# Convolution sums of VectorE in PSUM, and three tiles convolved on TensorE with streamed tap matrices of two token phases

## The chip, the cores and the metric

The kernel runs on one core of one Trainium2 chip. The metric is the device time of one execution in microseconds; less is better.

## What is computed

Two transformer blocks over 512 tokens of 1024 channels, in float32. The change lies in the second layer of the first block, a conformer convolution:

```python
def conformer_conv(h, w_pw1, b_pw1, w_dw, b_dw, ln_g, ln_b, w_pw2, b_pw2):
    u = h @ w_pw1 + b_pw1
    a, g = jnp.split(u, 2, axis=-1)
    u = a * jax.nn.sigmoid(g)
    u = depthwise_conv(u, w_dw) + b_dw
    u = jax.nn.silu(layer_norm(u, ln_g, ln_b))
    return u @ w_pw2 + b_pw2
```

The depthwise convolution has 31 taps along the tokens and its own weights for each channel. Before it stand an attention mixer and a squared-relu MLP, behind it another MLP and the second block with its gated MLP; they are the same in both kernels.

## The kernel before

Channels stand on the 128 partitions and the 512 tokens on the columns, so a tensor of 1024 channels is eight tiles. Each float32 operand of a product is split into a 12 bit head and the exact rest; a product of 128 input and 128 output channels is three TensorE instructions (`mm3`, L336 to L338): head by head, head by rest, rest by head.

Weights come from memory in the order of a plan (`make_plan`), packed into blocks of 512 columns; a load on SP's queue (L251) brings two blocks, 512 KB. ScalarE writes the head of each block (L264), VectorE the rest (L265), four blocks ahead of the one in use. Three buffers hold raw loads and nine hold split blocks. A raw buffer is free again when VectorE has split both its blocks.

The conformer's first product, `pw1`, gives two tiles of sums for each channel tile c, the value and the gate (24 instructions of 512 columns each); those of tiles 0 and 1 are computed in the part before. `glu` (L1131) evacuates them: two VectorE multiplications by the norm (L1136, L1137, one input in PSUM), a sigmoid on ScalarE, and one VectorE instruction that adds a bias and multiplies (L1139). Its result, with 15 zeros at each end, is convolved in one of four ways, by the letter in `CONV`:

- V (tiles 0, 2, 3): 31 VectorE instructions (L1087, then L1091), each of which multiplies the shifted input by a weight per partition and adds it to the sum. Input and sum are in SBUF.
- P (tiles 1, 4): for each tap ScalarE multiplies (L1102) and GpSimd adds (L1103), both in SBUF.
- M (tile 5): 10 taps as P and 21 as V into another buffer, and a VectorE addition of the two (L1171) at the end.
- E (tiles 6, 7): on TensorE. A tap is a diagonal matrix of 128 by 128, in head and rest, and 31 taps of three instructions of 512 columns add up in one bank of PSUM (`conv_pe` L1107 makes the head and rest of the input, L1109 and L1110, and `run_pe` L1114 issues the products). GpSimd writes the diagonals of tile 6 during the MLP before (L1056), ScalarE those of tile 7 as they are used (L1060).

V and P taps are background work: lists of closures of which a fixed number is issued at certain places of the program, from at most two tiles of a list in turn (`tick`, L318). `TICK = (5, 4)` is issued after each `pw1` product from tile 2's gate on (11 times): 5 taps of VectorE, 4 of ScalarE and GpSimd. `TICK2` is issued after every eight taps in `run_pe`. What is left comes after it (`drain`). Each engine works its instructions off in the order in which they were placed, so a split of weights stands behind the taps that were issued before it. PSUM has eight banks of 512 columns; all sums take theirs from these.

Behind the convolution comes the layer norm in halves of the tokens: TensorE sums all eight tiles over the partitions (`means`, L1179, in the order of `LN_ORDER`), ScalarE evacuates, VectorE subtracts, ScalarE squares, TensorE sums the squares (L1195).

Of the kernel before, what the change touches and what calls it, by code (L numbers as in the profile page):

```python
# [21 lines left out]
T = 512  # L22
# [10 lines left out]
CONV = "VPVVPMEE"  # L33
MIX = 10
TICK2 = (9, 5)
# [28 lines left out]
# ---------------------------------------------------------------- host layout  # L64


def vec_layout():
    cols, n = {}, 0
    for name, width in (("g", 64), ("sc", 12), ("qn", 3), ("kvn", 2), ("bp1", 16), ("dw", 248),
                        ("bdw", 8), ("lng", 8), ("lnb", 8), ("bp2", 8), ("n1", 8), ("n2", 8),  # L70
                        ("qn2", 1), ("kn2", 1), ("ps", 4), ("ifr", 1), ("sgn", 1)):
# [85 lines left out]
def pack(plan):  # L157
    """Cuts the plan into blocks of up to 512 columns, and those into loads of two blocks, but for the first two."""
# [7 lines left out]
    return [blocks[:1], blocks[1:2]] + [blocks[i:i + 2] for i in range(2, len(blocks), 2)]  # L166


def host_arrays(a):
# [7 lines left out]
    flat = lambda m: m.reshape(m.shape[0], -1)  # L177
    m = {
        "a": np.concatenate([win[:, 1536:2176], kr, kr, kr, krs], 1),
# [33 lines left out]
    ], 1)  # L213
# [10 lines left out]
# ---------------------------------------------------------------- chip  # L224


class Weights:
    """Streams the weight blocks in and splits each into a 12 bit head and the exact rest."""
# [40 lines left out]
    def more(self, limit):  # L269
        """Splits one block beyond what is due, up to a number of blocks ahead."""  # L270
# [12 lines left out]
class Program:  # L283
# [10 lines left out]
    # -- storage  # L294
# [23 lines left out]
    def tick(self, n, n2):  # L318
        """Background work: n and n2 operations of the two lists of queues, from a list's first two in turn."""
# [13 lines left out]
    # -- arithmetic  # L333
# [6 lines left out]
    def units(self, name, t, xs, ks=None):  # L340
        """One closure (ps, columns) per product of a weight piece."""
# [13 lines left out]
    def kouter(self, names, h, ps=None, cols=slice(0, T), hooks=None, extra=None, ks=None):  # L355
        """Several output tiles at once, an input tile after the other."""
# [13 lines left out]
    def split(self, p, src, scale=None, cols=T, rows=slice(0, 128)):  # L370
        """p = (head, rest) of src [* scale per partition]."""
# [12 lines left out]
    def rsqrts(self, jobs):  # L384
        """out = (s / n + eps) ** -0.5, with one Newton step, for each (s, n, out)."""
# [23 lines left out]
    # -- tables of the scalar engine  # L409
# [4 lines left out]
    def tables(self, name):  # L414
        """Has the scalar engine load a set of tables, behind the functions that need the one before."""
# [10 lines left out]
    def fn(self, name, **args):  # L426
        """An activation whose function needs a set of tables."""
# [6 lines left out]
    def colsum(self, acc, cols=T):  # L434
        """Sums of acc over the partitions, on every partition."""
# [19 lines left out]
    # -- constants  # L455
# [13 lines left out]
    def late_consts(self):  # L469
# [14 lines left out]
        # a query on the partitions, a key on the columns: later keys are out  # L484
# [4 lines left out]
        # a key on the partitions, a query on the columns: 32 queries before the first 96 keys,  # L489
        # which stand above the 32 keys before them  # L490
# [6 lines left out]
        # a key of the last 32 on the first partitions, a query on the columns  # L497
# [4 lines left out]
        # adds the second 32 partitions to the first  # L502
# [11 lines left out]
    def angles(self):  # L514
        """cos and sin of the rope angles, row p for frequency p % 16."""
# [23 lines left out]
    # -- attention parts that both blocks use  # L539
# [7 lines left out]
    def v_tile(self, ps, rows, scales=None):  # L547
        """Values of four (block, head) groups as [v | ones | v | ones ...], head and rest."""
# [19 lines left out]
    def max_rows(self, mx, q, rows):  # L568
        """Puts the negative of the row maxima (mx[:, 4 * head + block]) into a row of each q."""
# [61 lines left out]
    def normalise(self, e, o):  # L631
        """Values of a pair of heads over their sums: the even head is on top of its sums, the odd below."""
# [5 lines left out]
        # the negative of 1 / s, with one Newton step  # L638
# [8 lines left out]
    def head_ops(self, job, ys, nslots):  # L647
        """Closures for the scores and for the values of the slots of all heads; job(n) gives head n."""
# [20 lines left out]
    def parts(self, name, t, xs, done, ks=None, step=2):  # L669
        """A product in closures of a few input tiles each; done(sums) runs after the last."""  # L670
# [15 lines left out]
    # -- block 1, layer 0, mixer  # L686
    def mla(self, first):
# [10 lines left out]
        # products of constants until the first data is there: they raise the array's clock  # L698
# [68 lines left out]
        # shared key rope on partitions 64..95  # L767
# [6 lines left out]
        # query rope, (head, frequency) on the partitions  # L774
# [15 lines left out]
        # rows of a head: (64 | rope 32 | -max or 1 | zeros) or (-max or 1 | zeros | rope 32 | 64)  # L790
# [203 lines left out]
    # -- squared relu mlp  # L994
# [45 lines left out]
    # -- conformer convolution  # L1040
    def diagonals(self, c, early):
        """The taps of a channel tile as diagonal matrices, head and rest: at once, or eight as they are used."""
        nc = self.nc
        w = self.vec[:, self.V["dw"] + 31 * c:self.V["dw"] + 31 * c + 31]
        wh = self.cpool.tile([128, 32], F32R, name=f"wh{c}")
        wl = self.cpool.tile([128, 32], F32, name=f"wl{c}")
        nc.vector.tensor_copy(out=wh[:, :31], in_=w)
        nc.vector.tensor_sub(out=wl[:, :31], in0=w, in1=wh[:, :31].bitcast(F32))

        def eight(t0):  # L1050
            n = min(8, 31 - t0)
            pl = []
            for ww in (wh.bitcast(F32), wl):
                p = self.wide(F32R).rearrange("p (t c) -> p t c", c=128)
                if early:
                    nc.gpsimd.tensor_mul(out=p[:, :n], in0=self.ident[:, None, :].to_broadcast([128, n, 128]),  # L1056
                                         in1=ww[:, t0:t0 + n][:, :, None].to_broadcast([128, n, 128]))
                else:
# [17 lines left out]
    def conformer(self, x, h, ps4, rs, first):  # L1076
# [37 lines left out]
        def run_pe():  # L1114
            groups = [(i, t0) for i in range(len(late)) for t0 in range(0, 31, 8)]
            d, sums = {}, {}
            for n, (i, t0) in enumerate(groups):
# [4 lines left out]
                if t0 == 0:  # L1122
                    sums[i] = self.PS()
# [619 lines left out]
```

## Time and profile before

| | before |
|---|---|
| median of 3 timed runs | 1869.91 us (1869.52 to 1872.47) |
| span of the profiled execution | 1867.9 us |
| mean granted TensorE clock | 0.973 |
| TensorE busy | 1773.1 us, 95% |
| VectorE busy | 1176.0 us, 63% |
| ScalarE busy | 828.6 us, 44% |
| GpSimd busy | 330.1 us, 18% |

The profiled execution has its span as its time; it lies 2.0 us below the median of the timed runs. In the profile PE is TensorE's products and PEld its weight loads, DVE is VectorE, ACT ScalarE, POOL GpSimd and SP the engine whose queue issues the loads. A row of the timeline has the start and the duration in us, the engine, the line, the operation, the output and input tiles and how many instructions it merges; one of the lines by shape has the count, then busy us and mean ns of one, then the idle time before. [...]

### The profile page before, as it was taken

The page shows a single profiled execution, that of the slowest core. Times are in us where ns is not written, and L with a number is a line of the kernel's source. Part 1 is how long each engine was busy: PE and PEld are TensorE (multiplying, and loading weights), DVE is VectorE, ACT ScalarE, POOL GpSimd, SP SyncE. Part 2 cuts the span into 40 slices and gives each one's busy share as a digit, 9 for nine tenths or more (in the row PEclk, how much of TensorE's full clock was granted, in tenths as well). Part 3 has the DMA queues.
Part 4 walks back from the last instruction along what each step waited for, and adds up shares of the span by engine and source line. Part 5 has one row for each costly group of instructions (what it writes and reads, how often), then busy time and mean ns, then how long its engine had stood idle before and what let it go on. Part 6 is the DMA issues. An engine that isn't in the chain of part 4 may idle for free.

```text
span 1867.9 us, 22812 instructions
## 1 busy us (share of the span) xinstructions
PE 1773.1 (95%) x8630; PEld 1459.5 (78%) x8630; DVE 1176.0 (63%) x1786; ACT 828.6 (44%) x1531; POOL 330.1 (18%) x353
## 2 busy tenths in 40 slices
PE   9999979999999986839999999999999999999999
PEld 7778877888888865729888888887777888888887
DVE  7978695344444899985934443458988654344442
ACT  6546645333333544817644242436666433232231
POOL 3413270000000357820300000015122200000000
PEclk9999999999999998969999999999999999999999
DMA  5231313322222211002232232223221332332231
GB/s 200 70 96 50 102 46 113 99 93 90 101 92 79 86 39 55 14 22 69 91 100 94 90 102 90 93 87 104 59 81 53 117 102 90 94 98 91 93 99 57
DMA packets 47581, 158.83 MB, mean 85 GB/s; under 512 B 6592, under 2 KB 7040, under 8 KB 47472
## 3 DMA queue, kind: packets, MB, share of 16 engines
q1 hardware_dynamic: 45472, 152.31, 24.9%
q0 software_dynamic: 1936, 5.07, 0.9%
q8 instruction: 67, 1.10, 0.2%
q14 instruction: 42, 0.34, 0.1%
q10 hardware_dynamic: 64, 0.02, 0.0%
HBM read 149.86 MB, written 4.19 MB: 82 GB/s over the span
## 4 chain that ended last, share of the span: by engine, by line
PE 72%; DVE 20%; issue 3%; ACT 2%; POOL 1%; DMA 1%; SPq 0%; POOLq 0%; DVEq 0%; ACTq 0%
PE ps L337 23%; PE ps L336 23%; PE ps L338 23%; DVE P L1091 5%; DVE W L265 2%; DVE P L947 1%; DVE P L380 1%; DVE S L1091 1%; PE ps L602 1%; POOL P L950 1%; DVE S L1479 1%; ACT S L429 1%; DVE P L377 1%; DVE S L403 1%; PE ps L1195 1%
## 5 line engine op out<-in xcount | busy, mean ns | idle before, releaser
L338 PE MATMUL ps<-P,W 128*128 128x512 f32 (+1 forms) x2413 | 900.0, 373 | 16.6 <-DVE W L265 16.6
L337 PE MATMUL ps<-P,W 128*128 128x512 f32 (+1 forms) x2413 | 900.6, 373 | 8.5 <-DVE P L380 8.5
L336 PE MATMUL ps<-P,W 128*128 128x512 f32 (+1 forms) x2413 | 904.7, 375 | 2.2 <-ACT P L379 1.0
L265 DVE TENSOR_TENSOR W<-raw,W 128x512 fp32r<-128x512 f32 x546 | 399.0, 739 | 396.1 <-ACT W L264 391.9
L264 ACT ACTIVATE W<-raw 128x512 fp32r<-128x512 f32 x546 | 338.6, 629 | 681.0 <-PE ps L338 583.8
L338 PEld LDWEIGHTS ps<-P,W 128*128 128x128 f32 x2413 | 458.2, 190 | 105.4 <-DVE W L265 19.4
L337 PEld LDWEIGHTS ps<-P,W 128*128 128x128 f32 x2413 | 458.7, 190 | 95.1 <-DVE P L380 10.0
L336 PEld LDWEIGHTS ps<-P,W 128*128 128x128 f32 x2413 | 458.6, 190 | 90.2 <-ACT P L379 1.6
L950 POOL TENSOR_TENSOR P<-P 128x256 f32<-128x256 f32 x48 | 46.6, 979 | 798.7 <-DVE P L947 797.6
L377 DVE TENSOR_TENSOR P<-S,P 128x512 fp32r<-128x512 f32 (+1 forms) x130 | 91.0, 706 | 50.1 <-ACT P L376 49.3
L1103 POOL TENSOR_TENSOR P<-P,S 128x512 f32<-128x512 f32 x69 | 113.8, 1670 | 49.0 <-ACT S L1102 47.6
L1091 DVE SCALAR_TENSOR_TENSOR P<-P,vec 128x512 f32<-128x512 f32 x90 | 112.3, 1288 | 0.0
L376 ACT ACTIVATE P<-S 128x512 fp32r<-128x512 f32 (+1 forms) x130 | 78.9, 613 | 70.2 <-DVE S L1666 25.8
L1008 DVE SCALAR_TENSOR_TENSOR S<-ps,S 128x512 f32<-128x512 f32 x64 | 43.7, 690 | 37.3 <-PE ps L338 37.1
L379 ACT ACTIVATE P<-P,vec 128x256 fp32r<-128x256 f32 (+1 forms) x80 | 43.7, 550 | 50.3 <-POOL P L950 30.4
L449 POOL TENSOR_TENSOR S<-S 128x256 f32<-128x256 f32 (+1 forms) x45 | 48.1, 1070 | 76.3 <-ACT S L448 73.9
L380 DVE SCALAR_TENSOR_TENSOR P<-P,vec 128x256 fp32r<-128x256 f32 (+1 forms) x80 | 55.9, 712 | 8.3 <-ACT P L379 8.2
L336 PE MATMUL ps<-P 128*128 128x512 f32 (+4 forms) x134 | 53.0, 395 | 7.3 <-ACT P L1060 3.3
L337 PE MATMUL ps<-P 128*128 128x512 f32 (+4 forms) x134 | 53.3, 398 | 4.2 <-DVE P L1110 3.8
L338 PE MATMUL ps<-P 128*128 128x512 f32 (+4 forms) x134 | 52.9, 395 | 1.6 <-ACT P L1060 1.6
L615 POOL TENSOR_TENSOR P<-S,P 128x512 fp32r<-128x512 f32 (+1 forms) x24 | 34.3, 1428 | 112.5 <-DVE P L614 95.6
L448 ACT ACTIVATE S<-P 128x256 f32<-128x256 f32 (+1 forms) x105 | 46.4, 472 | 17.4 <-DVE P L1035 11.4
(270 smaller groups left out, 1464.2 us busy)
## 6 DMA issues: line engine op xcount, KB each, us to landing
raw<-in_w SPq DMA_DIRECT2D x270, 512.0 KB
P<-in_xT SPq DMA_DIRECT2D x8, 256.0 KB
P<-in_xT POOLq DMA_DIRECT2D x8, 256.0 KB, 5.7
keep<-P SPq DMA_DIRECT2D x8, 256.0 KB
P<-P SPq DMA_DIRECT2D x16, 128.0 KB
P<-keep POOLq DMA_DIRECT2D x8, 256.0 KB, 4.9
out<-P SPq DMA_DIRECT2D x7, 256.0 KB
raw<-in_w SPq DMA_DIRECT2D x2, 256.0 KB
```

The lines of the kernel that those rows point to most:

```text
L264: nc.scalar.activation(out=w[:, 0, :cols], in_=r, func=AF.Copy)
L265: nc.vector.tensor_sub(out=w[:, 1, :cols], in0=r, in1=w[:, 0, :cols].bitcast(F32))
L336: mm(ps, w[0], x[0], start=first, stop=False)
L337: mm(ps, w[0], x[1], start=False, stop=False)
L338: mm(ps, w[1], x[0], start=False, stop=last)
L376: nc.scalar.activation(out=hi, in_=src, func=AF.Copy)
L377: nc.vector.tensor_sub(out=lo, in0=src, in1=hi.bitcast(F32))
L380: nc.vector.scalar_tensor_tensor(out=lo, in0=src, scalar=scale, in1=hi.bitcast(F32), op0=OP.mult, op1=OP.subtract)
L449: (eng or nc.vector).tensor_add(out=acc, in0=acc, in1=t)
L950: ins = eng.tensor_add(out=x[k][:, cols], in0=x[k][:, cols], in1=m[k][:, cols]).ins
L1091: V.scalar_tensor_tensor(out=dst, in0=u, scalar=w, in1=dst, op0=OP.mult, op1=OP.add)
L1103: G.tensor_add(out=dst, in0=dst, in1=p)
```

## The change

- VectorE's sums (tiles V) are kept in a bank of PSUM; the last tap writes the result to SBUF.
- Tile 5 goes from M to E, so TensorE convolves three tiles, VectorE three, and GpSimd with ScalarE two.
- The E tiles use other matrices. The 128 partitions hold 64 channels at odd and at even tokens (two phases), and a matrix carries, for each pair of an input and an output phase, the tap that leads from the one to the other. 16 matrices, each on 256 columns, do the 31 taps of 64 channels. They are made on the host and come through the stream of weights between `pw1` and `pw2` (96 pieces of 128 columns). The diagonals, made on GpSimd and ScalarE, are gone.
- For that, the last step of `glu` of an E tile is four VectorE instructions of 64 partitions and 256 columns that read every second token, and its evacuation is four ScalarE instructions.
- `TICK2` goes from (9, 5) to (4, 2), issued after each of 12 groups of eight steps in place of eight groups of up to eight taps.

```diff
-CONV = "VPVVPMEE"
+CONV = "VPVVPEEE"
-TICK2 = (9, 5)
+TICK2 = (4, 2)
+EVEN_ODD = [c for c in range(8) if CONV[c] == "E"]
...
+    for i in range(2 * len(EVEN_ODD)):
+        kin("taps", i, range(16))
     kouter([("pw2", t) for t in range(4)])
...
+def tap_matrices(w):
+    m = np.zeros((16, 2, 64, 2, 64), np.float32)
+    ch = np.arange(64)
+    for s in range(16):
+        for a in range(2):
+            for b in range(2):
+                if 0 <= 2 * s + a - b < 31:
+                    m[s, a, ch, b, ch] = w[2 * s + a - b]
+    return m.reshape(16 * 128, 128)
...
         def conv_dve(c, up, dst, taps, bias):
...
                 if t == taps[0]:
+                    acc = box["acc"] = self.PS()
                     if bias:
-                        V.tensor_scalar(out=dst, in0=u, scalar1=w, scalar2=self.v("bdw", c), op0=OP.mult, op1=OP.add)
+                        V.tensor_scalar(out=acc, in0=u, scalar1=w, scalar2=self.v("bdw", c), op0=OP.mult, op1=OP.add)
...
-                    V.scalar_tensor_tensor(out=dst, in0=u, scalar=w, in1=dst, op0=OP.mult, op1=OP.add)
+                    acc = box["acc"]
+                    V.scalar_tensor_tensor(out=dst if dst is not None and t == taps[-1] else acc, in0=u, scalar=w,
+                                           in1=acc, op0=OP.mult, op1=OP.add)
...
-        def conv_pe(c, up):
-            uh, ul = self.wide(F32R)[:, :542], self.wide(F32R)[:, :542]
-            A.activation(out=uh, in_=up[:, :542], func=AF.Copy)
-            V.tensor_sub(out=ul, in0=up[:, :542], in1=uh.bitcast(F32))
+        def conv_pe(c, a, g):
+            up = self.wide(F32)[:, :544].rearrange("p (h t) -> p h t", h=2)
+            uh, ul = (self.wide(F32R)[:, :544].rearrange("p (h t) -> p h t", h=2) for _ in range(2))
+            G.memset(up[:, :, 0:8], 0.0)
+            G.memset(up[:, :, 263:272], 0.0)
+            a, g = (x.rearrange("p (t f) -> p f t", f=2) for x in (a, g))
+            for i in range(2):
+                r = slice(64 * i, 64 * i + 64)
+                for o, f, t in ((slice(0, 64), 1, 8), (slice(64, 128), 0, 7)):
+                    V.scalar_tensor_tensor(out=up[o, i, t:t + 256], in0=a[r, f], scalar=self.v("bp1", c)[r],
+                                           in1=g[r, f], op0=OP.add, op1=OP.mult)
+            A.activation(out=uh, in_=up, func=AF.Copy)
+            V.tensor_sub(out=ul, in0=up, in1=uh.bitcast(F32))
             late.append((c, uh, ul))
 
         def run_pe():
...
+            for i, (c, uh, ul) in enumerate(late):
+                sums = self.PS().rearrange("p (h t) -> p h t", h=2)
+                for g in range(2):
+                    for s in range(16):
+                        self.mm3(sums[:, g], W("taps", s, 2 * i + g), (uh[:, g, s:s + 256], ul[:, g, s:s + 256]),
+                                 s == 0, s == 15)
+                        if s % 8 == 7:
+                            self.tick(*TICK2)
+                out = vv[c].rearrange("p (t f) -> p f t", f=2)
+                for g in range(2):
+                    for b in range(2):
+                        r = slice(64 * b, 64 * b + 64)
+                        A.activation(out=out[64 * g:64 * g + 64, b], in_=sums[r, g], func=AF.Identity,
+                                     bias=self.v("bd2", 2 * i + g)[r])
...
-        with self.tc.issue_after(self.last_update):
-            self.conv_weights()
```

## Rows read from the trace of the kernel before

**Rows 1.** The page, part 4: the chain that ended last, by line.

```profile
PE ps L337 23%; PE ps L336 23%; PE ps L338 23%; DVE P L1091 5%; DVE W L265 2%; DVE P L947 1%; DVE P L380 1%; DVE S L1091 1%; PE ps L602 1%; POOL P L950 1%; DVE S L1479 1%; ACT S L429 1%; DVE P L377 1%; DVE S L403 1%; PE ps L1195 1%
```

**Rows 2.** Stretches: length, busy PE, PEld, DVE, ACT, POOL, PE clock, DMA share, GB/s.

```profile
660.00:670.00 10.00, 10.00 (x45) 8.10 (x44) 10.00 (x9) 7.23 (x12) 8.23 (x10) 1.00 0.00 0
690.00:700.00 10.00, 8.26 (x35) 6.42 (x35) 10.00 (x12) 4.25 (x7) 4.50 (x6) 1.00 0.17 52
810.00:820.00 10.00, 0.00 (x0) 0.00 (x0) 10.00 (x17) 0.00 (x0) 0.00 (x0) 0.50 0.00 0
860.00:870.00 10.00, 10.00 (x78) 9.64 (x77) 5.63 (x10) 8.89 (x17) 0.00 (x0) 1.00 0.59 177
```

**Rows 3.** Lines by shape, 640 to 830 us: count, busy us, mean ns, idle before.

```profile
L1103 POOL TENSOR_TENSOR P<-P,S 128x512 f32<-128x512 f32 x69 | 113.8, 1670 | 49.0 <-ACT S L1102 47.6
L1091 DVE SCALAR_TENSOR_TENSOR P<-P,vec 128x512 f32<-128x512 f32 x90 | 112.3, 1288 | 0.0
L265 DVE TENSOR_TENSOR W<-raw,W 128x512 fp32r<-128x512 f32 x30 | 27.7, 950 | 0.1
L1136 DVE TENSOR_TENSOR S<-ps,S 128x512 f32<-128x512 f32 x8 | 5.4, 678 | 0.0
L1060 ACT ACTIVATE P<-ident,wh 128x128 fp32r<-128x128 f32 x31 | 9.5, 387 | 0.0
```

**Rows 4.** Timeline of VectorE: start us, us, line, operation.

```profile
661.49 1.80 DVE L1091 SCALAR_TENSOR_TENSOR P<-P,vec 128x512 f32<-128x512 f32 x1
...
804.95 1.75 DVE L1091 SCALAR_TENSOR_TENSOR S<-P,vec,S 128x512 f32<-128x512 f32 x1
806.62 0.74 DVE L1091 SCALAR_TENSOR_TENSOR P<-P,vec 128x512 f32<-128x512 f32 x1
807.28 0.74 DVE L1091 SCALAR_TENSOR_TENSOR S<-P,vec,S 128x512 f32<-128x512 f32 x1
...
827.15 0.68 DVE L1171 TENSOR_TENSOR P<-P,S 128x512 f32<-128x512 f32 x1
```

**Rows 5.** Timeline of VectorE and GpSimd, 742 to 753 us.

```profile
742.87 3.44 DVE L265 TENSOR_TENSOR W<-raw,W 128x512 fp32r<-128x512 f32 x2
...
749.95 3.05 POOL L1103 TENSOR_TENSOR P<-P,S 128x512 f32<-128x512 f32 x1 [2.51 <-ACT S L1102]
...
750.57 1.28 DVE L265 TENSOR_TENSOR W<-raw,W 128x512 fp32r<-128x512 f32 x2
...
751.77 0.67 DVE L1136 TENSOR_TENSOR S<-ps,S 128x512 f32<-128x512 f32 x1
...
752.38 0.67 DVE L1137 TENSOR_TENSOR S<-ps,S 128x512 f32<-128x512 f32 x1
```

**Rows 6.** Timeline of TensorE, products of 256 columns and a weight load.

```profile
644.05 0.28 PE L336 MATMUL ps<-P,W 128*128 128x256 f32 x1
...
644.17 0.28 PE L337 MATMUL ps<-P,W 128*128 128x256 f32 x1
644.17 0.19 PEld L338 LDWEIGHTS ps<-P,W 128*128 128x128 f32 x1
```

**Rows 7.** Timeline and chain, 827 to 852 us: means (L1179) and squares (L1195).

```profile
827.28 2.07 PE L1179 MATMUL ps<-P,onesf 128*128 128x256 f32 x4 [19.86 <-DVE P L1091]
...
830.86 6.64 PE L1195 MATMUL ps<-S,onesf 128*128 128x256 f32 x16 [1.50 <-ACT S L1194]
...
848.65 3.50 PE ps L1195 x16
```

**Rows 8.** VectorE's lines by shape: forms near the new ones.

```profile
L380 DVE SCALAR_TENSOR_TENSOR P<-ps,vec,P 128x512 fp32r<-128x512 f32 x4 | 2.8, 747 | 0.0
...
L947 DVE SCALAR_TENSOR_TENSOR P<-P,vec,S 128x256 f32<-128x256 f32 x1 | 0.5, 472 | 0.0
```

**Rows 9.** Waits from 650 to 832 us (total, times, longest), and GpSimd's timeline.

```profile
POOL P L1103 <- ACT S L1102: 47.6, 11, 19.1
...
262.21 2.08 POOL L1056 TENSOR_TENSOR P<-ident,wh 128x1024 fp32r<-128x1024 f32 x1
```

More of the change, by code (lines that the diff above doesn't have):

```diff
@@ L177, in host_arrays @@
     flat = lambda m: m.reshape(m.shape[0], -1)
+    dw, bdw = f("odd_w_dw")[0], f("odd_b_dw")[0]
+    halves = [slice(128 * c + 64 * g, 128 * c + 64 * g + 64) for c in EVEN_ODD for g in range(2)]
     m = {
+        "taps": np.concatenate([tap_matrices(dw[:, r]) for r in halves], 1),
         "a": np.concatenate([win[:, 1536:2176], kr, kr, kr, krs], 1),
@@ L212, in host_arrays @@
         np.tile(np.repeat(np.array([-1.0, 1.0], np.float32), 16), 4)[:, None],
-    ], 1)
+    ] + [np.tile(bdw[r], 2)[:, None] for r in halves], 1)
     return {
@@ L1038, in mlp @@
         return self.boundary(x, m, macc, last, gi, nxt, first, extra)
[L1041 to L1058, printed above, removed]
-                    for i in range(n):
-                        nc.scalar.activation(out=p[:, i], in_=self.ident, func=AF.Copy,
-                                             scale=ww[:, t0 + i:t0 + i + 1])
-                pl.append(p)
-            return [(pl[0][:, i], pl[1][:, i]) for i in range(n)]
-        if early:
-            d = sum([eight(t) for t in range(0, 31, 8)], [])
-            self.diag[c] = lambda t0: d[t0:t0 + 8]
-        else:
-            self.diag[c] = eight
-    def conv_weights(self):
-        self.diag = {}
-        for n, c in enumerate(c for c in range(8) if CONV[c] == "E"):
-            self.diagonals(c, n == 0)
     def conformer(self, x, h, ps4, rs, first):
         nc = self.nc
-        V, A, G, mm = nc.vector, nc.scalar, nc.gpsimd, nc.tensor.matmul
+        V, A, G, mm, W = nc.vector, nc.scalar, nc.gpsimd, nc.tensor.matmul, self.W
         vv = self.pairs()
@@ L1082, in conv_dve @@
         def conv_dve(c, up, dst, taps, bias):
+            box = {}
             def tap(t):
@@ L1112, in conv_pe @@
             late.append((c, uh, ul))
         def run_pe():
-            groups = [(i, t0) for i in range(len(late)) for t0 in range(0, 31, 8)]
-            d, sums = {}, {}
-            for n, (i, t0) in enumerate(groups):
-                for g in groups[:n + 3]:
-                    if g not in d:
-                        d[g] = self.diag[late[g[0]][0]](g[1])
-                c, uh, ul = late[i]
-                if t0 == 0:
-                    sums[i] = self.PS()
-                for j, dd in enumerate(d[i, t0]):
-                    t = t0 + j
-                    self.mm3(sums[i], dd, (uh[:, t:t + T], ul[:, t:t + T]), t == 0, t == 30)
-                self.tick(*TICK2)
-                if t0 == 24:
-                    A.activation(out=vv[c], in_=sums[i], func=AF.Identity, bias=self.v("bdw", c))
+            for i, (c, uh, ul) in enumerate(late):
[12 more added lines that the diff above has]
+                                     bias=self.v("bd2", 2 * i + g)[r])
@@ L1138, in glu @@
             self.fn(SIGMOID, out=g, in_=g, func=AF.Sigmoid, bias=self.v("bp1", 8 + c))
+            if CONV[c] == "E":
+                return conv_pe(c, a, g)
+            up = self.wide(F32)
+            G.memset(up[:, 0:15], 0.0)
+            G.memset(up[:, 527:542], 0.0)
             V.scalar_tensor_tensor(out=up[:, 15:527], in0=a, scalar=self.v("bp1", c), in1=g,
@@ L1143, in glu @@
             elif CONV[c] == "V":
-                self.bg.append(conv_dve(c, up, vv[c], range(31), True))
-            elif CONV[c] == "M":
-                part = self.S()[:, :T]
+                self.bg.append(conv_dve(c, up, vv[c], range(31), True)[0])
+            else:
                 self.bg2.append(conv_pool(c, up, vv[c], range(MIX)))
-                self.bg.append(conv_dve(c, up, part, range(MIX, 31), False))
+                taps, part = conv_dve(c, up, None, range(MIX, 31), False)
+                self.bg.append(taps)
                 mixed.append((c, part))
-            else:
-                conv_pe(c, up)
         za = self.PS()
@@ L1170, in conformer @@
         for c, part in mixed:
-            V.tensor_add(out=vv[c], in0=vv[c], in1=part)
+            V.tensor_add(out=vv[c], in0=part["acc"], in1=vv[c])
         self.tables(RSQRT)
```

9 lines of the change are left out of this document (3 added, 6 removed).

## The prediction

> **What bounds the kernel now.** I read the page's chain by line first: TensorE's three product lines carry 23% each, and the largest VectorE line is the tap of the convolution, L1091, with 5% and 1% [rows 1]. Then the stretches around those taps: from 661 to 827 us VectorE is busy in every microsecond, while TensorE falls to 8.26 of 10 us at 690 and to nothing at 810 [rows 2]. So this stage is VectorE's, and what the change is worth is read there; elsewhere TensorE bounds and nothing is touched.
>
> Why VectorE is so long there is in the lines by shape and the timeline. A tap has a mean of 1288 ns [rows 3], but that is a mix: while GpSimd adds, taps follow each other every 1.67 us (804.95 to 806.62); once its last add is over, every 0.66 us (806.62 to 807.28) [rows 4]. The splits of weights (L265) show the same: a pair took 3.44 us at 742.87 and 1.28 us at 750.57 [rows 5]. So a VectorE instruction with both inputs in SBUF and a GpSimd add exclude each other, at 1.67 - 0.66 = 1.01, say 1.04 us a meeting. An instruction with one input in PSUM does not: at 751.77 and 752.38 L1136 and L1137 ran at 0.61 us a start beside an add that lasted from 749.95 to 753.00 [rows 5]. That add stood still beside the pair of splits and, once it was free at 751.77, needed 1.23 us.
>
> Check of the reading: from 661.49 to 827.75 there are 166.3 us. At uncontended rates the queue holds 113 taps at 0.66 (74.6), 17 splits at 0.60 (10.2), ten L1136/L1137 at 0.60 (6.0), five gates at 0.66 (3.3), two rests of E tiles (1.3) and L1171 (0.6): 96.0. The missing 70.3 us over 69 adds [rows 3] is 1.02 us an add. Nearly every add meets a tap.
>
> **The change, part by part**, VectorE from 661.49 [rows 4] on:
> - Taps: tile 5 is no longer convolved here, so 92 remain of 113. Input and sum are now SBUF and PSUM. No row shows VectorE writing PSUM. Nearest rows: 0.66 us for a tap with everything in SBUF [rows 4], 0.75 for a scalar_tensor_tensor with a PSUM input [rows 8]; far end 1.67. I take 0.66 where taps of two tiles alternate (72) and the whole 0.75 for the last 20, where tile 3 stands alone and each tap needs the one before: 47.5 + 15.0 = 62.5. [...]
> - Splits: 17 as now, the last two at 750.57 [rows 5], and 24 more, since 96 tap matrices of 128 columns are 24 blocks of 512: 41 x 0.60 = 24.6.
> - Gates: ten L1136/L1137, 6.0; two whole gates, 1.3; for tiles 5 to 7 four quarter gates each, bounded by the 256 column form at 0.47 [rows 8] and, should the stride of two cost double, 0.94: 12 x 0.47 = 5.6 (up to 11.2); three rests, 1.9.
> - Sum without any meeting: 101.9 us, end at 763.4. That is more than the 96.0 of now: all the gain must come from adds that no longer meet a tap.
> - Meetings left: 58 instructions with two SBUF inputs (41 splits, 2 + 12 gates, 3 rests), 60 adds. Bounds 0 and 58 x 1.04 = 60.3. Five pairs of splits now lie beside a running add (the last at 742.87 and 750.57, [rows 5]); they lost 2.2, 1.1, 2.2, 2.2 and 0, in the mean 1.5, which is half an add for the first and a whole one for the second. GpSimd waits 28.5 us for ScalarE after its first add (47.6 less 19.1, [rows 9]) of some 143, so it is busy 0.8 of the time; in the convolution two adds of 1.23 in a tick of about 4.2 us make 0.6. So 8.5 pairs x 1.56 x 0.8 = 10.6; two gates, 0.8; three E tiles x (0.52 + 3 x 1.04 + 0.52) x 0.8 = 10.0; 12 pairs x 1.56 x 0.6 = 11.2; together 32.6. VectorE ends at 796.0.
> - TensorE: a 512 column product starts every 0.23 us (45 touch the 10 us from 660, [rows 2]), a 256 column one every 0.12 (644.05 to 644.17, [rows 6]; 0.118 over a longer stretch). 240 products of tiles 3 to 7 are 55.7, the convolution goes from 186 x 0.23 = 43.2 to 288 x 0.118 = 34.0. From 658.5 that is 748.2, so TensorE waits for VectorE, not the reverse. Its weight loads of 0.19 us lie beside the products at that pace [rows 6].
> - ScalarE loses 62 diagonals (19.0 us, [rows 3]), 10 tap products, gains 24 heads; it is off the path before and after. GpSimd loses eight products of 2.1 us at 262 [rows 9], which lie beside TensorE's MLP: nothing. Its chain is the next one late: 60 adds at the 1.65 us of now [rows 3] and the 28.5 us of waits end at 789.
> - SP's queue gains 12 loads of 512 KB, behind pw1's and ahead of pw2's. Each needs a buffer that VectorE's splits free. 6.3 MB in about 47 us is 134 GB/s, below the 177 of another stretch [rows 2], so I put no wait here; at TensorE's own pace it would be 185 and would bind.
> - PSUM: two or three of the eight banks hold sums for long; four for two pairs of gate sums remain. Nothing, unless a bank comes free late.
> - Behind VectorE's end: four quarter evacuations of the last tile at about 0.4 (128 columns took 387 ns, [rows 3]) and the means of four channels, 1.8, and 1.6 of products: 5 us. Now the means end at 827.28 + 2.07 = 829.35 [rows 7]. After: 801.0, that is 28.3 sooner. [...] TensorE now works up to the end, so I count these 3.1 too.
>
> Sum: 31.4 us less than the profiled execution's span of 1867.9, or 1836.5; the median of the timed runs lies 2.0 above that span, so 1838 us.
>
> **Rivals.**
> - Adds and splits rarely meet: splits that fall in GpSimd's gaps, or GpSimd that stands back as at 749.95 [rows 5]. The end is then near 763.4 + 5, and 64.1 us go: 1806. For it: one of five pairs lost nothing. Against: three lost everything. Between 1806 and 1824: chance 0.25.
> - Every one of the 58 meets a whole add: 823.7 + 5, only 3.8 us gained, 1866. For it: now nearly every add meets one. [...] Between 1850 and 1866: 0.13.
> - Slower: the sum in PSUM is the mechanism, at L1091's successor. If reading and writing one bank costs more than 1.0 us a tap (0.66 + 31.4 / 92), the gain is gone; at the 1.67 of now's contended taps it would be 93 us more, 1931. For it: no row shows the write. Against: L1136 and the 747 ns of [rows 8]. 0.06.
> - The change doesn't do what it says: products of 256 columns wait for their weights (the load's 0.19 instead of 0.118). 288 x 0.19 = 55 us from about 741, where the gates end, is 796: a tie with VectorE, some 3 us at most. [Rows 6] speak against it. That the tap matrices arrive late (24 blocks at half of 134 GB/s, 47 us more) would give 1885, chance under 0.02.
>
> **The numbers.** My own case, 1824 to 1850, has 0.5; with the rivals' share the range 1808 to 1862 leaves out under 2 in 10: the lower end is no meeting, the upper nearly all. A measurement of this kernel tells 0.2%, 3.7 us, from no change. Faster 0.89, within 0.05 (the all-meeting case and late matrices in part), slower 0.06.
>
> **What would show it.** Right: taps of a mean near 0.7 us also beside adds, adds near 1.3 instead of 1.65 us, splits with a mixed mean near 1.2 us, VectorE still without idle time up to about 796, TensorE's products of the convolution 0.118 apart within a group but in bursts, the means at a granted clock near 1. Wrong: taps above 1 us; ScalarE's heads of the tap matrices waiting on loads; GpSimd's last add, not VectorE's last tap, ahead of the means; TensorE without a gap in the convolution, which would be the first rival.

## The result and the profile after

| | before | after |
|---|---|---|
| median of the timed runs | 1870.91 us, 4 runs (1869.52 to 1872.47) | 1823.59 us, 4 runs (1821.01 to 1825.19) |
| ratio after to before | | 0.9745, interval 0.9731 to 0.9759 |
| span of the profiled execution | 1867.9 us | 1823.5 us |
| mean granted TensorE clock | 0.973 | 0.983 |
| TensorE busy | 1773.1 us, 95% | 1753.0 us, 96% |
| VectorE busy | 1176.0 us | 1126.3 us |
| GpSimd busy | 330.1 us | 289.0 us |

The change is faster by 47.3 us, inside the range of the prediction and 14.4 us below its 1838. In the changed kernel the lines have other numbers: L1079 is the tap, L1092 GpSimd's add, L283 the split, L282 its head on ScalarE, L1107 the quarter gate, L1110 the rest of an E tile, L1177 and L1193 the means and squares, L354 to L356 TensorE's products.

The chain by line of the kernel after (part 4 of the page) answers to [rows 1]: TensorE's shares have grown from 23 to 24%, and the tap has fallen from 5 and 1% to 3%.

```profile
PE ps L355 24%; PE ps L354 24%; PE ps L356 24%; DVE W L283 3%; DVE ps L1079 3%; DVE P L965 1%; PE ps L620 1%; DVE P L398 1%; DVE P L1107 1%; DVE P L395 1%; POOL P L968 1%; ACT S L447 1%; PE ps L1193 1%; DVE S L421 1%; DVE S L1477 1%
```

The stretches of the kernel after answer to [rows 2] (length, then busy PE, PEld, DVE, ACT, POOL, PE clock as a share of full speed, DMA share, GB/s).

```profile
260.00:280.00 20.00, 20.00 (x129) 18.13 (x129) 18.20 (x34) 11.60 (x24) 3.59 (x4) 1.00 0.44 140
...
660.00:670.00 10.00, 10.00 (x45) 8.10 (x44) 10.00 (x15) 4.05 (x8) 4.53 (x5) 1.00 0.16 54
690.00:700.00 10.00, 8.97 (x39) 6.96 (x37) 9.89 (x12) 4.88 (x8) 7.92 (x6) 1.00 0.12 47
720.00:730.00 10.00, 3.77 (x28) 3.27 (x26) 9.96 (x13) 2.78 (x5) 6.07 (x5) 0.84 0.15 52
...
780.00:790.00 10.00, 5.17 (x11) 3.67 (x12) 5.98 (x13) 3.15 (x9) 0.00 (x0) 0.50 0.17 52
```

VectorE is still busy in nearly every microsecond of the convolution, and TensorE still waits for it: 3.77 of 10 us at 720. So the bound of the stage is the one of before; it is shorter. VectorE now puts 15 instructions into 660 to 670 where it had 9. The first row is of another place, and it was a surprise: the same 20 us of the kernel before are

```profile
260.00:280.00 20.00, 13.96 (x80) 11.98 (x78) 19.93 (x15) 5.06 (x11) 17.90 (x10) 0.91 0.16 53
```

There TensorE stood for 6 of 20 us, beside GpSimd's diagonals. The forecast had called this stretch free.

The lines by shape of the kernel after, 640 to 830 us, answer to [rows 3]: count, busy us, mean ns, idle before.

```profile
L1092 POOL TENSOR_TENSOR P<-P,S 128x512 f32<-128x512 f32 x60 | 89.5, 1505 | 39.4 <-ACT S L1091 37.1
L1079 DVE SCALAR_TENSOR_TENSOR ps<-P,vec,ps 128x512 f32<-128x512 f32 x87 | 61.0, 744 | 0.1
L283 DVE TENSOR_TENSOR W<-raw,W 128x512 fp32r<-128x512 f32 x57 | 53.6, 967 | 2.4 <-ACT W L282 2.2
...
L1107 DVE SCALAR_TENSOR_TENSOR P<-S,vec 64x256 f32<-64x256 f32 x12 | 14.1, 1171 | 0.1
```

A tap has 744 ns in place of 1288. The splits and quarter gates, which still have two inputs in SBUF, pay for GpSimd's adds now: 967 and 1171 ns, against 718 and 481 in experiment 4, which leaves nearly all adds out. VectorE's timeline answers to [rows 4].

```profile
651.75 0.75 DVE L1079 SCALAR_TENSOR_TENSOR ps<-P,vec,ps 128x512 f32<-128x512 f32 x1
...
749.51 2.38 DVE L283 TENSOR_TENSOR W<-raw,W 128x512 fp32r<-128x512 f32 x2
751.82 2.72 DVE L1079 SCALAR_TENSOR_TENSOR ps<-P,vec,ps 128x512 f32<-128x512 f32 x4
...
780.96 1.53 DVE L1079 SCALAR_TENSOR_TENSOR ps<-P,vec,ps 128x512 f32<-128x512 f32 x2
782.53 0.75 DVE L1079 SCALAR_TENSOR_TENSOR P<-P,vec,ps 128x512 f32<-128x512 f32 x1
```

GpSimd's timeline in the same stretch, and VectorE's next split:

```profile
746.49 15.10 POOL L1092 TENSOR_TENSOR P<-P,S 128x512 f32<-128x512 f32 x9
...
754.45 2.37 DVE L283 TENSOR_TENSOR W<-raw,W 128x512 fp32r<-128x512 f32 x2
```

GpSimd adds without a pause from 746.49 to 761.59. In that time four taps take 2.63 us (751.82 to the next split at 754.45), 0.66 each from start to start, as without adds, where one that lasts 0.74 us is followed by the next after 0.66 (806.62 to 807.28, [rows 4]): here a tap that sums in PSUM is not slowed by them. A pair of splits takes 2.31 us (749.51 to 751.82) against 1.20 for the pair at 750.57 before the change (to 751.77, [rows 5]). TensorE's means and squares answer to [rows 7].

```profile
783.33 2.07 PE L1177 MATMUL ps<-P,onesf 128*128 128x256 f32 x4 [6.45 <-DVE P L1079]
786.91 6.70 PE L1193 MATMUL ps<-S,onesf 128*128 128x256 f32 x16 [1.50 <-ACT S L1192]
```

TensorE waited 6.45 us for VectorE's last tap, and its squares still ran at a granted clock of 0.50 (780 to 790), as in 810 to 820 before the change [rows 2], and took 6.70 us against 6.64 [rows 7].

**Where the 44.4 us between the two spans came from.** From the first tap to the end of the first means it was 660.37 to 829.35, 169.0 us; now it is 650.38 to 785.40, 135.0: 34.0 us. The first tap comes 10.0 us sooner, at 650.38. What follows the means is 0.4 us shorter. The first of these three is the forecast's; the second is not in it.

### The profile page after: what moved, and what is told of

Its sections match the earlier page's. It is cut to its first block, busy times and chain, and to the rows that moved or that the text cites. A ratio compares the mean times of both kernels' runs of the same rounds, so it can differ in the third digit from the quotient of the medians.

```text
span 1823.5 us, 23018 instructions
## 1 busy us (share of the span) xinstructions
PE 1753.0 (96%) x8732; PEld 1456.5 (80%) x8732; DVE 1126.3 (62%) x1794; ACT 823.2 (45%) x1494; POOL 289.0 (16%) x336
## 4 chain that ended last, share of the span: by engine, by line
PE 75%; DVE 16%; issue 4%; ACT 2%; POOL 1%; DMA 0%; SPq 0%; POOLq 0%; ACTq 0%; DVEq 0%
PE ps L355 24%; PE ps L354 24%; PE ps L356 24%; DVE W L283 3%; DVE ps L1079 3%; DVE P L965 1%; PE ps L620 1%; DVE P L398 1%; DVE P L1107 1%; DVE P L395 1%; POOL P L968 1%; ACT S L447 1%; PE ps L1193 1%; DVE S L421 1%; DVE S L1477 1%
## 5 line engine op out<-in xcount | busy, mean ns | idle before, releaser
L356 PE MATMUL ps<-P,W 128*128 128x512 f32 (+2 forms) x2509 | 926.9, 370 | 24.4 <-DVE W L283 24.4
L354 PE MATMUL ps<-P,W 128*128 128x512 f32 (+2 forms) x2509 | 930.7, 371 | 4.3 <-ACT W L282 2.0
L355 PE MATMUL ps<-P,W 128*128 128x512 f32 (+2 forms) x2509 | 926.4, 369 | 6.1 <-DVE P L398 6.1
L283 DVE TENSOR_TENSOR W<-raw,W 128x512 fp32r<-128x512 f32 (+1 forms) x570 | 418.7, 743 | 397.9 <-ACT W L282 394.1
L282 ACT ACTIVATE W<-raw 128x512 fp32r<-128x512 f32 (+1 forms) x570 | 352.7, 628 | 676.5 <-PE ps L356 587.4
L356 PEld LDWEIGHTS ps<-P,W 128*128 128x128 f32 (+1 forms) x2509 | 477.4, 190 | 112.0 <-DVE W L283 28.1
L355 PEld LDWEIGHTS ps<-P,W 128*128 128x128 f32 (+1 forms) x2509 | 478.0, 191 | 90.6 <-DVE P L398 7.2
L354 PEld LDWEIGHTS ps<-P,W 128*128 128x128 f32 (+1 forms) x2509 | 477.6, 190 | 89.9 <-ACT W L282 2.6
L968 POOL TENSOR_TENSOR P<-P 128x256 f32<-128x256 f32 x48 | 46.6, 979 | 801.5 <-DVE P L965 800.5
L1092 POOL TENSOR_TENSOR P<-P,S 128x512 f32<-128x512 f32 x60 | 89.5, 1505 | 39.4 <-ACT S L1091 37.1
L1079 DVE SCALAR_TENSOR_TENSOR ps<-P,vec,ps 128x512 f32<-128x512 f32 x87 | 61.0, 744 | 0.1
L467 POOL TENSOR_TENSOR S<-S 128x256 f32<-128x256 f32 (+1 forms) x45 | 48.1, 1069 | 76.8 <-ACT S L466 74.4
L466 ACT ACTIVATE S<-P 128x256 f32<-128x256 f32 (+1 forms) x105 | 46.4, 473 | 17.4 <-DVE P L1053 11.3
L1046 DVE TENSOR_TENSOR P<-ps,P 128x512 f32<-128x512 f32 x42 | 29.0, 692 | 30.9 <-PE ps L356 30.9
L620 PE MATMUL ps<-P 128*128 128x512 f32 (+3 forms) x160 | 41.3, 376 | 1.2 <-DVE S L1443 0.8
L447 ACT ACTIVATE S<-ps 128x512 f32<-128x512 f32 (+2 forms) x56 | 31.8, 579 | 20.2 <-PE ps L623 9.6
```

The lines of the kernel that those rows point to most:

```text
L282: nc.scalar.activation(out=w[:, 0, :cols], in_=r, func=AF.Copy)
L283: nc.vector.tensor_sub(out=w[:, 1, :cols], in0=r, in1=w[:, 0, :cols].bitcast(F32))
L354: mm(ps, w[0], x[0], start=first, stop=False)
L355: mm(ps, w[0], x[1], start=False, stop=False)
L356: mm(ps, w[1], x[0], start=False, stop=last)
L620: mm(o[:m], k, q[:, pl, c0:], start=n == 0 and m == 128, stop=n == len(keys) - 1 and mask is None)
```

## The experiments

The ratios below are to the kernel before, run on the same chip: 1869.74 us for the first four, 1869.23 for the next four, 1869.89 for the last two. Beside the changed kernel it took 1870.91, so a difference in us between the changed kernel and an experiment is uncertain by some 2 us.

**1. GpSimd's diagonals put back at their old place, unused.** This adds work to the changed kernel that nothing reads.

```diff
+        with self.tc.issue_after(self.last_update):
+            self.diagonals_unused(6)    # eight tensor_mul of 128x1024 on GpSimd
```

> The changed kernel, with the eight GpSimd products that wrote tile 6's diagonals (L1056 of before) put back at their old place, some 262 us from the start; nothing uses what they write. Theory: each of them holds VectorE's next instruction with two SBUF inputs for some 2 us there, TensorE waits for those, and the 10 us by which the changed kernel enters the convolution earlier (first tap at 650.4 instead of 660.4 us) come from their absence. Then the time rises from 1823.6 by 10 to 14 us, to 1834 to 1838, and the span of TensorE without work around 262 to 290 us comes back. Rival, as I had forecast: they lie beside TensorE's products and cost nothing; then 1822 to 1826, and the 10 us have another cause.

Measured: 1833.55 us (1832.90 to 1836.73), ratio 0.9808 (0.9792 to 0.9824): 10.0 us more than without them. The stretch of the experiment at 260 us and VectorE's timeline there:

```profile
260.00:280.00 20.00, 14.90 (x80) 12.92 (x78) 19.93 (x15) 5.10 (x11) 17.95 (x10) 0.83 0.16 53
```

```profile
262.49 2.12 DVE L467 TENSOR_TENSOR S<-S 128x256 f32<-128x256 f32 x1
264.53 2.38 DVE L283 TENSOR_TENSOR W<-raw,W 128x512 fp32r<-128x512 f32 x1
266.84 2.11 DVE L398 SCALAR_TENSOR_TENSOR P<-P,vec 128x256 fp32r<-128x256 f32 x1
268.87 2.11 DVE L467 TENSOR_TENSOR S<-S 128x256 f32<-128x256 f32 x1
```

Each VectorE instruction there lasts as long as one of GpSimd's products, 2.0 to 2.4 us, where the same line takes 0.41 (L467, at 266.07) or 0.68 (L283, at 264.59) in the changed kernel without those products. Eight instructions of some 4 us in all take 16.7 (262.49 to 279.18). TensorE waits for them, by way of ScalarE and directly. In the kernel before, these are among the waits from 240 to 300 us (total, times, longest):

```profile
ACT P L376 <- DVE S L449: 15.7, 2, 14.3
...
PE ps L337 <- DVE P L380: 5.4, 2, 3.7
```

TensorE's two waits there are

```profile
268.96 0.39 PE L337 MATMUL ps<-P,W 128*128 128x256 f32 x1 [3.71 <-DVE P L380]
...
281.65 0.79 PE L438 MATMUL ps<-P,ones 128*128 128x512 f32 x1 [3.98 <-ACT P L376]
```

They make 7.7 us, and they are not the whole price: behind each of them TensorE's mean granted clock was lower for a while, 0.66 in 270 to 275 and 0.54 in 280 to 285, where the changed kernel has 1.00 from 260 to 300. So about 10 of the 47.3 us are the diagonals'. They were not hidden.

**2. The sums back in SBUF,** all else as changed.

```diff
-                    acc = box["acc"] = self.PS()
+                    acc = box["acc"] = dst
```

> The changed kernel, with VectorE's convolution sums in SBUF again; tiles, tap matrices and ticks stay as changed. Theory: every one of GpSimd's 60 adds then meets a VectorE instruction, at about 1.02 us, in place of the some 30 us of meetings that are left now, so that VectorE's convolution ends 25 to 33 us later: 1849 to 1857 us; taps of two mixed durations, 0.74 and 1.75. Rival: the gain comes from tile 5's move to TensorE, and PSUM matters little: 1824 to 1830 us.

Measured: 1853.63 us (1852.48 to 1855.28), ratio 0.991 (0.9896 to 0.9925): 30.0 us more. The lines by shape, as above:

```profile
L1079 DVE SCALAR_TENSOR_TENSOR P<-P,vec 128x512 f32<-128x512 f32 x90 | 96.4, 1109 | 0.2
L1092 POOL TENSOR_TENSOR P<-P,S 128x512 f32<-128x512 f32 x60 | 95.1, 1596 | 58.5 <-ACT S L1091 56.4
```

The tap rises from 744 to 1109 ns; the 90 taps take 96.4 us in place of 63.2 (61.0 for 87, 2.2 for the three that write the result), 33.2 more, of which 30.0 show in the time. Only the place of the sum differs, so the bank of PSUM is the mechanism of this part.

**3. The sums in PSUM alone,** in the kernel before; tiles, diagonals and ticks as before.

```diff
-                        V.tensor_scalar(out=dst, in0=u, scalar1=w, scalar2=self.v("bdw", c), op0=OP.mult, op1=OP.add)
+                        V.tensor_scalar(out=acc, in0=u, scalar1=w, scalar2=self.v("bdw", c), op0=OP.mult, op1=OP.add)
...
-                    V.scalar_tensor_tensor(out=dst, in0=u, scalar=w, in1=dst, op0=OP.mult, op1=OP.add)
+                    V.scalar_tensor_tensor(out=dst if t == taps[-1] else acc, in0=u, scalar=w, in1=acc,
+                                           op0=OP.mult, op1=OP.add)
```

> The kernel before, with only VectorE's sums moved to PSUM; diagonals, four kinds of tiles and ticks as before. Theory: VectorE's queue needs 96 us uncontended and some 20 us of meetings with splits and gates; GpSimd's 69 adds at about 1.5 us and 28 us of waits end at about 790, later than VectorE. So the convolution ends 35 to 42 us sooner than before, and the time is 1828 to 1836: more than the whole gain of the stage in the changed kernel, without any new matrices. Rival: the tap in PSUM needs TensorE's third tile to pay; then under 20 us gained, above 1850.

Measured: 1813.67 us (1811.32 to 1815.56), ratio 0.9695 (0.9681 to 0.971). Both expectations missed: this one edit is faster than the whole change, by 9.9 us, though it keeps the diagonals at 262 us and their 10. GpSimd's and VectorE's lines by shape, then their last instructions of the convolution and TensorE's means and squares:

```profile
L1108 POOL TENSOR_TENSOR P<-P,S 128x512 f32<-128x512 f32 x69 | 96.7, 1424 | 34.1 <-ACT S L1107 32.7
L1095 DVE SCALAR_TENSOR_TENSOR ps<-P,vec,ps 128x512 f32<-128x512 f32 x106 | 71.8, 745 | 0.0
```

```profile
772.99 0.74 DVE L1095 SCALAR_TENSOR_TENSOR P<-P,vec,ps 128x512 f32<-128x512 f32 x1
...
771.22 4.66 POOL L1108 TENSOR_TENSOR P<-P,S 128x512 f32<-128x512 f32 x3 [0.85 <-ACT S L1107]
...
773.56 3.94 PE L1184 MATMUL ps<-P,onesf 128*128 128x256 f32 x16
779.00 3.72 PE L1200 MATMUL ps<-S,onesf 128*128 128x256 f32 x16 [1.50 <-ACT S L1199]
```

The stage, from the first tap at 662.67 to the end of the means at 777.50, is 114.8 us, 20.2 less than with the whole change. VectorE's queue explains it. From the first to the last tap it takes 111.1 us here and 132.9 with the change, 21.8 more. By busy time the change adds 24.1 us of splits (45 with 45.9 us against 17 with 21.8) and 14.1 of quarter gates, and takes off 12.2 of taps (93 against 114); three whole gates and tile 5's addition less (3.7) and a rest more (1.9) leave 24.2, and part of that overlaps. VectorE alone no longer sets the end here: its last tap ends at 773.73 and GpSimd's last add at 775.88, and the last means wait for the add. The expectation had this order, with GpSimd at about 790. And TensorE, with no wait ahead of its means, runs the squares in 3.72 us in place of 6.70.

**4. The changed kernel without 58 of its 60 adds.** The sums of GpSimd's tiles are left out but for the last product, so its output is not the convolution's.

```diff
-                G.tensor_add(out=dst, in0=dst, in1=p)
+                if t == 30:
+                    G.tensor_add(out=dst, in0=dst, in1=p)
```

> The changed kernel without 58 of GpSimd's 60 additions in the convolution (tiles 1 and 4 are thus not convolved; the rest is as it is). Theory: the some 30 us that VectorE still loses to meetings go, its queue of 102 us ends at about 754 instead of 783 us, and TensorE's products end not before 740: 26 to 30 us less, 1793 to 1798 us. Rival: loads of the tap matrices or ScalarE's heads bind behind VectorE: 10 to 18 us less, 1805 to 1814, with VectorE idle in the convolution.

Measured: 1800.75 us in a single run, between the two expectations. VectorE's last tap ended at 761.1 from a first tap at 650.17, 110.9 us against 132.9: 22.0 us are the meetings, judged by the end alone. A line by shape from 640 to 830 us and a wait from 650 to 790 us (total, times, longest):

```profile
L283 DVE TENSOR_TENSOR W<-raw,W 128x512 fp32r<-128x512 f32 x64 | 44.1, 718 | 8.7 <-ACT W L282 8.5
```

```profile
DVE W L283 <- ACT W L282: 3.9, 3, 3.2
```

The split is at 718 ns, the quarter gate at 481; but now VectorE waits for ScalarE's heads, 3.9 us of it up to 790. Part of what the meetings gave back went into this new wait. From its second tap on VectorE's queue took 109.6 us against the 101.9 of the forecast's sum without meetings; the wait and four splits more than forecast (2.4) make 6.3 of these 7.7.

**5. The quarter gates relieved:** the gate's first value stays in its bank of PSUM, so that each gate has one input in SBUF.

```diff
-            a, g = self.S()[:, :T], self.S()[:, :T]
+            a, g = za, self.S()[:, :T]
```

> The changed kernel, with the value of the gate (times the norm) written back to its bank of PSUM instead of to SBUF, so that the quarter gates of the E tiles have one SBUF input. Theory: the twelve quarter gates, 1171 ns each in the changed kernel because they meet adds, fall to some 480; VectorE, which sets the end of the convolution, ends 6 to 9 us sooner: 1814 to 1818 us. Rival: the adds merely meet the next instruction instead, or loads bind: within 2 us of 1823.6.

Measured: 1814.18 us (1811.74 to 1816.44), ratio 0.9702 (0.9688 to 0.9717), as expected: 9.4 us less than the changed kernel. The line is now

```profile
L1107 DVE SCALAR_TENSOR_TENSOR P<-ps,vec,S 64x256 f32<-64x256 f32 x12 | 5.8, 482 | 0.1
```

so 12 x (1171 - 482) ns = 8.3 us of the 14.1 were meetings. The stride of two costs next to nothing: 482 ns stand beside the 472 of a 256 column form without it [rows 8].

**6. A fourth tile on TensorE,** on top of experiment 5, which takes one more tile from VectorE.

```diff
-CONV = "VPVVPEEE"
+CONV = "VPEVPEEE"
```

> As e5, and tile 2 goes from VectorE to TensorE, so that four tiles are convolved with tap matrices. Theory: VectorE loses 31 taps of 0.66 (20.5 us) and gains 8 splits at 1.02, a rest and three quarter gates (some 11.5 us); TensorE has 11.3 us more but waits for VectorE now. So another 6 to 11 us sooner than e5: 1804 to 1811 us. Rival: the loads of the tap matrices and ScalarE's heads bind behind VectorE, as some 3 us at a time showed without the adds: no gain over e5.

Measured: 1814.39 us (1814.36 to 1819.15), ratio 0.971 (0.9695 to 0.9725): no gain, a miss. Among the waits from 640 to 790 us is

```profile
ACT W L282 <- DMA raw<-in_w: 19.4, 9, 4.3
```

ScalarE's heads wait for weights, and VectorE for the heads (8.3 us). The rival had said that the loads bind.

**7. PSUM alone, the diagonals issued later.** The edit of experiment 3 with the order of issue tied to a later ScalarE square.

> The kernel before with VectorE's sums in PSUM (as e3), and GpSimd's eight products for tile 6's diagonals held back until the first square of the MLP's first chunk is done, where VectorE is busy less than half of the time and TensorE has split blocks ahead. Theory: the 10 us at 262 us go, as putting them back into the changed kernel cost 10.0: 1801 to 1806 us against 1813.7 of e3. Rival: they delay VectorE's splits there as much and TensorE waits again: 1811 to 1815 us.

Measured: 1812.51 us (1810.66 to 1814.95), ratio 0.9696 (0.9681 to 0.9712): nothing. The edit did not do what it was to do. GpSimd's timeline:

```profile
262.48 2.08 POOL L1056 TENSOR_TENSOR P<-ident,wh 128x1024 fp32r<-128x1024 f32 x1
...
275.24 1.86 POOL L1056 TENSOR_TENSOR P<-ident,wh 128x896 fp32r<-128x896 f32 x1
282.04 1.81 POOL L1056 TENSOR_TENSOR P<-ident,wl 128x896 fp32r<-128x896 f32 x1 [4.94 <-PE ps L439]
```

Seven of the eight stayed where they were, and only the last one waited. The order of issue made no wait here; this says nothing on the theory.

**8. The changed kernel with tile 5 mixed again** (and the ticks of before), the matrices of tiles 6 and 7 streamed.

```diff
-CONV = "VPVVPEEE"
+CONV = "VPVVPMEE"
-TICK2 = (4, 2)
+TICK2 = (9, 5)
```

> The changed kernel with tile 5 split between GpSimd and VectorE again (M) and the old ticks of (9, 5); tiles 6 and 7 keep the streamed tap matrices. Theory: a tile with tap matrices costs VectorE 8 splits and a rest at the price of meetings and four quarter gates, some 14 us, about what its 21 taps cost; so 1820 to 1828 us, and what the changed kernel loses against PSUM alone (1823.6 against 1813.7 less the 10 of the diagonals) lies in the tap matrices of tiles 6 and 7, not in tile 5's move. Rival: tile 5's move is the loss: 1802 to 1812 us.

Measured: 1824.37 us (1823.41 to 1828.41), ratio 0.9761 (0.9746 to 0.9776), the time of the whole change. So the loss against PSUM alone is not in the move of tile 5 but in the streamed matrices of the E tiles, with the loads, splits and quarter gates that they bring. Its quarter gates:

```profile
L1107 DVE SCALAR_TENSOR_TENSOR P<-S,vec 64x256 f32<-64x256 f32 x8 | 9.3, 1164 | 0.1
```

**9. PSUM alone, the diagonals held back by data:** VectorE's copy of the taps reads the last hidden tile of the MLP's first half (times zero), so that GpSimd cannot start before it.

```diff
-        nc.vector.tensor_copy(out=wh[:, :31], in_=w)
+        nc.vector.scalar_tensor_tensor(out=wh[:, :31], in0=self.hid0, scalar=0.0, in1=w, op0=OP.mult, op1=OP.add)
...
+                               mid=self.conv_weights)
```

> The kernel before with the sums of VectorE's convolution in PSUM (113 taps, matrices and tiles of before), and its eight diagonal products of 128x1024 on GpSimd moved from the first MLP (262 us) to the end of that MLP's first half, by data: VectorE's copy of the taps now also reads the last tile of the hidden layer. Theory (the 10 us at 262 us are GpSimd's diagonals against VectorE's two-SBUF-input work, which TensorE there waits for; where TensorE has a lead they cost nothing): TensorE busy 20.0 of 20 us in 260 to 280, 1801 to 1806 us, the fastest of all the kernels here. Rival (wherever they stand they delay VectorE, and TensorE waits for it a little later): 1811 to 1815, the gap in TensorE's work only moved.

Measured: 1802.39 us (1798.34 to 1803.85), ratio 0.9632 (0.9615 to 0.9649), the fastest full computation of the series, 11.3 us below experiment 3 and 21.2 below the change. The stretches and GpSimd's timeline:

```profile
260.00:280.00 20.00, 19.55 (x130) 18.02 (x131) 18.21 (x35) 12.12 (x25) 3.92 (x5) 1.00 0.39 127
...
300.00:320.00 20.00, 20.00 (x87) 16.20 (x86) 9.44 (x8) 6.82 (x11) 15.56 (x8) 1.00 0.24 79
```

```profile
298.36 1.94 POOL L1057 TENSOR_TENSOR P<-ident,wh 128x1024 fp32r<-128x1024 f32 x1 [30.68 <-PE ps L338]
300.27 2.34 POOL L1057 TENSOR_TENSOR P<-ident,wl 128x1024 fp32r<-128x1024 f32 x1
...
313.44 2.12 POOL L1057 TENSOR_TENSOR P<-ident,wl 128x896 fp32r<-128x896 f32 x1
```

The same eight products of about 2 us now lie at 298 to 316, where TensorE has a lead: it is busy 20.00 of 20 us, and VectorE has only eight instructions there. They cost nothing where nothing waits, and 11 us where the next product needs VectorE. From the first tap on experiments 3 and 9 take the same 1150.4 us, so all of the difference lies ahead of the convolution.

**10. A fourth load buffer** for experiment 6, with seven scratch tiles in place of nine.

```diff
-    RAW = 3
+    RAW = 4
```

> The kernel with four tiles on TensorE by streamed tap matrices and the gate's value in PSUM (1814.4 us), with four load buffers of 512 columns in place of three, and seven scratch tiles in place of nine to make room. Theory 1 (the loads are late there because each waits for a buffer that a split frees): the wait of ScalarE's heads for loads shrinks from 19.4 us to under 10, 1804 to 1810 us. Theory 2 (the loads themselves bind: 8.4 MB in the stage at some 200 GB/s): 1812 to 1817, the wait stays near 19 us.

Measured: 1809.54 us (1807.51 to 1813.82), ratio 0.968 (0.9664 to 0.9697). The wait for loads, as in experiment 6:

```profile
ACT W L282 <- DMA raw<-in_w: 3.6, 3, 2.1
```

It shrinks from 19.4 to 3.6 us, and the time by 4.9, with intervals that just touch (0.9695 and 0.9697). So most of that wait was for a free buffer and not for the rate of the loads, which reached 194 GB/s (740 to 760). The heads now wait 6.1 us for TensorE, and TensorE 11.8 for the splits; what bounds the rest was not tested.

## Why the prediction was right, and where it was off

The direction and the mechanism in the convolution were right; the sum was 13.0 us short. The time lies in the range, but 0.4 us outside the prediction's own case (1824 to 1850) and inside the band of its first rival (1806 to 1824), and not for that rival's reason: adds and splits did meet. With the diagonals back in their place (experiment 1) it is 1833.6, well within the own case. By its steps, against the 31.4 us that it took off the span (44.4 came off):

- **The bound of the stage** was VectorE, before and after: right.
- **The tap in PSUM** at 0.66 to 0.75 us: right, 744 ns and 0.66 from start to start beside adds. Experiment 2 shows the cause: 30.0 us go when the sums return to SBUF. The row that was nearest to a write into PSUM was the right one to take, and the rival with 1.67 us a tap fell. The runs show 0.66 us from start to start with the sum in PSUM (751.82 to 754.45 for four) and with everything in SBUF (806.62 to 807.28, [rows 4]) alike. The 0.75 us put on the last 20 taps came only where two of one sum followed each other, 0.785 us; most of them stood between splits, at 0.66.
- **Sum without meetings and 32.6 us of meetings**, together 134.5 us: measured 651.75 to 783.28, 131.5, that is 3.0 less. By the means of the lines the meetings were 45 splits x (1042 - 678) ns = 16.4 (45 in the stage, mean 1042 there), 12 quarter gates x 689 = 8.3 and three rests, 1809 ns each against an estimate of 720 from the split's 678, 3.3: 28.0. The forecast had 21.8 for the splits and 10.0 for the E tiles. So an intermediate share of meetings was the right choice between rivals 1806 and 1866, and the mechanism of neither came. Without the meetings that leaves 103.5 us against the forecast's 101.9, as 45 splits stood in the stage and not 41. The adds took 1505 ns, not the 1.3 us of the signs, since they still met splits and gates; and GpSimd's chain ended at 761.59, 27 us before its forecast of 789 (10 of them the earlier first tap), off the path. Experiments 2, 3 and 5 agree with the forecast's reading that a VectorE instruction with two inputs in SBUF and GpSimd's add exclude each other and that one with a single input there does not: taps took 1109 ns with both inputs in SBUF, 744 and 745 with one in PSUM, and the quarter gates 1171 against 482.
- **Five us behind VectorE's end:** 2.1 measured (783.28 to 785.40). The picture was wrong. It put an E tile's evacuations last; TensorE's products ended at 773.3, and VectorE's own third tile, its last tap at 782.53, came last. The gain is 2.9.
- **3.1 us from the squares,** the distance of the first half's 6.64 us from the second's 3.50 [rows 7]: no run of the changed kernel shows this term. They took 6.70 us, at a granted clock of 0.50 (780 to 792), and TensorE had again stood for 6.45 us ahead of the means. In experiment 3, where it did not stand, they took 3.72 at 1.00 (780 to 790). The term was right in size (6.70 - 3.72 = 3.0), its condition ("TensorE now works up to the end") was not met.
- **"GpSimd loses eight products of 2.1 us at 262, which lie beside TensorE's MLP: nothing."** This is the step that failed, together with "elsewhere TensorE bounds and nothing is touched". They cost 10.0 us (experiment 1) to 11.3 (experiment 9 against 3), which the forecast put at nothing. The same exclusion that the forecast had worked out for the convolution was not applied to a product on GpSimd in another stage, where it holds a VectorE instruction for its whole 2 us (2.11 for one that takes 0.41 without it, experiment 1), and where TensorE waits for that instruction (3.71 us, and 3.98 by way of ScalarE, before the change).

3.0 + 2.9 - 3.1 + 10.0 make 12.8 of the 13.0 us. That the errors of the second and third term cancel is luck.

- **The loads** of 512 KB at 134 GB/s, "no wait": right for the time, as VectorE had no idle; ScalarE's heads waited 14.0 us for loads off the path; the prediction had named such waits, for the tap matrices, as a sign of being wrong. It binds once VectorE has less to do (experiment 6: 19.4 us of waits for loads).
- **TensorE's 256 column products:** 0.12 from start to start while their matrices are there and the granted clock is at 1.00 (772.07 to 773.04 for eight); behind the longer waits 0.21 (715.54 to 720.23 for 22), at a granted clock of 0.50. Of TensorE's 24.4 us of waits for splits 20.7 were ahead of these products, which is VectorE's time again.

What the forecast did not ask is which part of the change earns the gain. The PSUM sums earn more than all of it; the rest of the change loses 21.2 us against diagonals that are kept out of the way (experiment 9), 22.0 with tile 5 left as it was (experiment 8), for 28 more splits and 12 quarter gates on the engine that bounds the stage.

The traces bear out the diagonals' price. From GpSimd's first L950 (L968) to the first tap it is 424 to 427 us in the four traces with the diagonals at their old place (before, experiments 1, 3 and 7) and 412 to 416 in the eight others. Between the changed kernel and experiment 1 that stretch differs by 13.0 us (412.8 against 425.8). The changed kernel's starts 3.6 us later, and what follows its first tap is 1.7 longer, which leaves the 7.7 between the two spans. One thing stays open: the start of that stretch lies between 233.9 and 239.4 us in the twelve traces, by a difference earlier on that was not traced; no run was made for it.

## What to carry to other kernels

Where two engines exclude each other on SBUF, try to put the operand that one of them rereads, a running sum above all, into PSUM: in experiment 3 114 taps then ran beside 69 adds at 0.66 us a start. Before calling a removed or moved piece of work hidden, ask not only which engine it is on but which other it holds, and whether anything waits for that one there. Try the parts of a change singly: here one of them alone (experiment 3, 56.1 us) was worth more than the whole (47.3).

## What the runs showed that was not expected

- A VectorE tap that sums into PSUM costs the same as one into SBUF that meets no add, 0.66 us from start to start for 512 columns (751.82 to 754.45 for four, against 806.62 to 807.28 before the change, [rows 4]). Two taps of the same sum, back to back, take 0.785 each (780.96 to 782.53 for two); with another instruction between them, such as a split, nothing of that is left: 0.66 from a tap at 765.84 to the split at 766.50.
- An instruction of 256 columns (L467) that takes 0.41 us in the changed kernel took 2.11 in experiment 1, beside GpSimd products of 1024 columns that took 16.46 us for eight: there the price of a meeting was set by the length of the other engine's instruction, not of VectorE's own.
- A wait of 6.45 us just ahead of the last means went with squares at a granted clock of 0.50 (6.70 us), while without one they ran at 1.00 (3.72 in experiments 3 and 9). In experiment 6 they took 3.73, at 1.00 as well, behind a wait of 4.7 us.
